# Two-layer decoder trunk: gate and up projections as block products with seven multiplications

## The chip, the cores and the metric

The kernel runs on one core of a Trainium2 chip. The metric is the device time of one execution in microseconds, as the median of several runs. Five engines work side by side: TensorE (PE, matmuls; its weight loads are listed as PEld), VectorE (DVE), ScalarE (ACT), GpSimd (POOL) and SyncE (SP), whose queue issues almost all the transfers of this kernel.

## The reference

The trunk has two layers on 1024 tokens of width 1024, in float32. Each layer is a mixer and a feed-forward block, each behind a root-mean-square norm and with its result added to x. The mixer of layer 0 is two gated convolutions, that of layer 1 a gated linear recurrence and a dilated attention. The feed-forward block is the part that the change is about:

```python
def conv_glu_ffn(h, w_gate, w_up, conv_w, conv_b, w_down):
    g = causal_dwconv(h @ w_gate, conv_w) + conv_b
    return (jax.nn.silu(g) * (h @ w_up)) @ w_down
```

with h of 1024 x 1024, `w_gate` and `w_up` of 1024 x 2816, `w_down` of 2816 x 1024, and a causal convolution of three taps over the tokens.

## The kernel before

Everything is kept channel-major: channels lie on the 128 partitions, tokens in the free dimension. A projection is therefore cut into tiles of 128 output channels, a contraction over 8 tiles of 128 channels (`KD`), and two halves of 512 tokens, since one PSUM bank holds 512 columns.

Each product is made of three matmuls. A float32 operand is split into a high part (a cast by ScalarE, L124 or L190) and a low part (a subtraction by VectorE, L125 or L191), and high x high, high x low and low x high are added up in PSUM (`in_part`, `in_full`, `out_pair`). All matmuls go through `mm` (L165). The weights are fetched in units of 128 x 1024 by `fetch` (L113) into two raw buffers and split by `load_w` into eight weight tiles.

`Norm` keeps x times the gain split in `hT`; 1 / rms is computed beside it (`stat`, `prep`, `spread`) as a row `br` that is multiplied into the results of the first projections.

A feed-forward layer (`ffn`, L317) goes over 22 channel tiles f. For each it runs the gate unit and the up unit (`in_unit`), then `evac` (L322): the multiplication by `br` (L324), bias and first tap (L325), two more taps (L301), silu (L327), again `br` (L328, on GpSimd), the multiplication by the up result (L329), and the split of the activation into two tiles of the g pool. The down projection is woven in: after each chunk of two tiles f, the activations of the chunk before are multiplied with their rows of `w_down` by eight `out_pair`, which add into x (L281). So neither activations nor x leave SBUF; only between layer 0 and layer 1 is x stored to `xscr` and read back later.

The order on each engine is not the order in which the lines are written. A planner at compile time goes through all instructions, knows their dependences and priorities (an earlier line has the higher one), and puts the next ready one on each engine. A buffer pool with n slots lets the planner run ahead by n tiles. Pools that are closed give their place to pools opened later, and a new tile then waits for the last use of the tile that it lies on.

Of the kernel before, what the change touches and what calls it, by code (L numbers as in the profile page):

```python
# [29 lines left out]
# columns of the packed per-channel parameters  # L30
# [11 lines left out]
# order of the packed weight units  # L42
# [9 lines left out]
def trunk(ctx, tc, x, wpk, par, wgate, masks, ident, out):  # L52
# [3 lines left out]
    hpool = ctx.enter_context(tc.tile_pool(name="hpool", bufs=4))  # L56
    wpool = ctx.enter_context(tc.tile_pool(name="wpool", bufs=8))
    rpool = ctx.enter_context(tc.tile_pool(name="rpool", bufs=2))
    gpool = ctx.enter_context(tc.tile_pool(name="gpool", bufs=8))
    xpool = ctx.enter_context(tc.tile_pool(name="xpool", bufs=2))  # L60
    dpool = ctx.enter_context(tc.tile_pool(name="dpool", bufs=1, space=bass.MemoryType.DRAM))
# [6 lines left out]

    def g_tile(dt=F32):
        return gpool.tile([P, 1024], dt, tag="g", name=nm("g"))  # L70
# [14 lines left out]

    def open_e(st):
        E["e"] = st.enter_context(tc.tile_pool(name=nm("ep"), bufs=7, reuse_waits="tile"))
        E["b"] = st.enter_context(tc.tile_pool(name=nm("bp"), bufs=1, reuse_waits="tile"))

    def open_psum(st, mm_bufs, tr_bufs):  # L90
        E["mm"] = st.enter_context(
            tc.tile_pool(name=nm("mmp"), bufs=mm_bufs, space=bass.MemoryType.PSUM, reuse_waits="tile"))
        trp = st.enter_context(
            tc.tile_pool(name=nm("trp"), bufs=tr_bufs, space=bass.MemoryType.PSUM, reuse_waits="tile"))
        E["tr"] = lambda shape: trp.tile(shape, F32, tag="tr", name=nm("tr"))

# [7 lines left out]

    st = ExitStack()
    open_e(st)
    open_psum(st, 3, 2)

    raws = {}

    def fetch(u):
        raw = rpool.tile([P, 1024], F32, tag="raw", name=nm("raw"))
        nc.sync.dma_start(raw, wpk[u])  # L113
        return raw

    def w_tile():
        return wpool.tile([P, 1024], F32R, tag="w", name=nm("w"))
# [16 lines left out]
    raw0 = raws[U_EVIN] = rpool.tile([P, 1024], F32, tag="raw", name=nm("raw"))  # L134
# [21 lines left out]
    xscr = dpool.tile([2, P, KD, 512], F32, name="xscr")  # L156
# [3 lines left out]
    def new_hT():  # L160
        return [[hpool.tile([P, KD, 512], F32R, tag="hT", name=nm("hT")) for _ in range(2)]
                for _ in range(2)]
# [5 lines left out]
    def colvec(sm, nt, scale):  # L168
        """(scale * column sums + eps) ** -0.5 by token, tokens on partitions."""
# [12 lines left out]
    class Norm:  # L182
        def __init__(self, n, xs, hT):
            self.n, self.xs, self.hT, self.acc, self.rs, self.br = n, xs, hT, {}, {}, None

        def turn(self, hf, ks):
            hi, lo = self.hT[hf]
            for k in ks:
                xk, g = self.xs[hf][:, k, :], pc("ng", 8 * self.n + k)
                nc.scalar.activation(hi[:, k, :], xk, AF.Identity, scale=g)  # L190
                nc.vector.scalar_tensor_tensor(  # L191
                    lo[:, k, :], xk, g, hi[:, k, :].bitcast(F32), ALU.mult, ALU.subtract)

        def stat(self, hf, cp):
            sq = e_tile()
            nc.scalar.activation(sq.rearrange("p (a b) -> p a b", a=2),  # L196
                                 self.xs[hf][:, 2 * cp:2 * cp + 2, :], AF.Square)
            if cp == 0:
                self.acc[hf] = sq
            else:  # L200
                nc.gpsimd.tensor_add(self.acc[hf], self.acc[hf], sq)  # L201

        def prep(self, hf):
            sm = self.acc[hf]
            nc.gpsimd.tensor_add(sm[:, 0:512], sm[:, 0:512], sm[:, 512:1024])
            self.rs[hf] = rs = colvec(sm, 4, 1.0 / D)
            self.dg = e_tile()
            diag(self.dg, rs, 4)

        def spread(self, hf):  # L210
            ps = tr_tile([P, 512])
            mm(ps, one1, self.dg[:, 0:512], True, True)
            if hf == 0:
                self.br = E["b"].tile([P, 1024], F32, tag="br", name=nm("br"))
            nc.scalar.copy(self.br[:, hf * 512:(hf + 1) * 512], ps)

        def stats(self):
            for hf in range(2):
                for cp in range(4):
                    self.stat(hf, cp)  # L220

        def hooks(self):
            """By half, unit and contraction tile of the first projections."""
            return {(0, 2, 4): lambda: self.prep(0), (1, 0, 0): lambda: self.spread(0),
                    (1, 0, 4): lambda: self.prep(1), (1, 1, 2): lambda: self.spread(1)}

# [1 line left out]
    def in_part(ps, w, hT, hf, hook):  # L228
        wh, wl = w
        hi, lo = hT[hf]  # L230
        o = ps[:, hf * 512:(hf + 1) * 512]
        for k in range(KD):
            hook(k)
            c = slice(k * P, (k + 1) * P)
            mm(o, wh[:, c], hi[:, k, :], k == 0, False)
            mm(o, wl[:, c], hi[:, k, :], False, False)
            mm(o, wh[:, c], lo[:, k, :], False, k == KD - 1)

    def in_full(ps, w, hT):
        wh, wl = w  # L240
        for k in range(KD):
            c = slice(k * P, (k + 1) * P)
            for hf in range(2):
                o = ps[:, hf * 512:(hf + 1) * 512]
                mm(o, wh[:, c], hT[hf][0][:, k, :], k == 0, False)
                mm(o, wh[:, c], hT[hf][1][:, k, :], False, False)
            for hf in range(2):
                o = ps[:, hf * 512:(hf + 1) * 512]
                mm(o, wl[:, c], hT[hf][0][:, k, :], False, k == KD - 1)

    def in_first(units, norm):
        hooks = norm.hooks()
# [30 lines left out]
    def out_one(xs, hf, c, t0, n, parts):  # L283
        o = mm_tile()[:, :n]
        t = slice(hf * 512 + t0, hf * 512 + t0 + n)
        cs = slice(c * P, (c + 1) * P)
        for i, ((ah, al), (wh, wl)) in enumerate(parts):
            mm(o, wh[:, cs], ah[:, t], i == 0, False)
            mm(o, wh[:, cs], al[:, t], False, False)
            mm(o, wl[:, cs], ah[:, t], False, i == len(parts) - 1)  # L290
        xv = xs[hf][:, c, t0:t0 + n]
        nc.vector.tensor_add(xv, xv, o)

    def out_all(xs, parts):
        for hf in range(2):
            for cp in range(4):
                out_pair(xs, hf, cp, parts)

# [3 lines left out]

    def r_tile():
        return g_tile(F32R)

    def out_norm(xs, parts, norm, before=None):
        """Last output projection of a phase with the next phase's norm behind it."""
        for hf in range(2):
            for cp in range(4):
                out_pair(xs, hf, cp, parts)  # L310
                if before:
                    before(hf, cp)
                norm.turn(hf, (2 * cp, 2 * cp + 1))
                norm.stat(hf, cp)

# [1 line left out]
    def ffn(layer, xs, norm, finish):  # L317
        hT = norm.hT
        u0 = U_F[layer]
        chunks = [list(range(2 * c, 2 * c + 2)) for c in range(9)] + [list(range(18, 22))]  # L320

        def evac(f, pg, pu):  # L322
            g, t = e_tile(), e_tile()
            nc.vector.tensor_mul(g, norm.br, pg)  # L324
            nc.scalar.activation(t, g, AF.Identity, bias=pc(f"fb{layer}", f), scale=pc(f"fw{layer}", 44 + f))  # L325
            conv_rest(t, g, lambda i: pc(f"fw{layer}", 22 * i + f), 3)
            nc.scalar.activation(t, t, AF.Silu)  # L327
            nc.gpsimd.tensor_mul(t, t, norm.br)  # L328
            nc.vector.tensor_mul(t, t, pu)  # L329
            return split(t, r_tile)  # L330

        def down(acts):
            return [(a, load_w(u0 + 44 + f)) for f, a in acts.items()]

        pend = None
        for ci, ch in enumerate(chunks):
            acts = {}
            for n, f in enumerate(ch):
                if ci == 0 and n == 0:
                    pg, pu, pg1 = in_first([u0 + 0, u0 + 1, u0 + 2], norm)  # L340
                    acts[0] = evac(0, pg, pu)
                elif ci == 0:
                    acts[1] = evac(1, pg1, in_unit(u0 + 3, hT))
                else:
                    pg = in_unit(u0 + 2 * f, hT)
                    pu = in_unit(u0 + 2 * f + 1, hT)
                    acts[f] = evac(f, pg, pu)
                if n == 1 and pend is not None:
                    out_all(xs, down(pend))
            pend = acts  # L350
        return finish(down(pend))
# [702 lines left out]
```

## Time and profile before

| | us |
|---|---|
| median of 3 runs | 2322.82 (2322.39 to 2324.06) |
| span of the profiled execution | 2320.8 |
| TensorE busy in it | 2238.9 |
| VectorE busy | 1245.4 |
| ScalarE busy | 667.4 |
| GpSimd busy | 452.8 |

The profiled execution has no run time of its own in the page; its span, from the first to the last instruction, is 2.0 us under the median, and the difference is what lies around the instructions. In the span, the first mixer lasts to about 402 us, the first feed-forward to about 1123 us, the mixer of layer 1 to about 1585 us, and the second feed-forward to the end.

How to read it: the busy time of an engine is the time in which at least one of its instructions was in flight. The chain that ended last is followed back from the last instruction, at each step to what released it. A bracket behind a row says how long the engine was idle before it and what ended that.

### The profile page before, as it was taken

What the parts mean: (1) busy time and instruction counts of PE and PEld (TensorE: products, weight loads), DVE (VectorE), ACT (ScalarE), POOL (GpSimd) and SP (SyncE); (2) the same over time, 40 slices, a digit from 0 to 9 for tenths busy, and PEclk for the clock granted to TensorE, in tenths of its full rate; (3) what the DMA queues carried; (4) which work ended last, traced back from release to release, by engine and by line L of the source; (5) the groups of instructions that cost most, each with busy time, mean ns of one, the idle gap of its engine ahead of it and who ended that gap; (6) DMA issues with size and microseconds to landing.
All of it is one profiled execution on the core that took longest, in us unless ns stands there. A gap on an engine that the chain in (4) does not pass through costs nothing.

```text
span 2320.8 us, 26137 instructions
## 1 busy us (share of the span) xinstructions
PE 2238.9 (96%) x11064; PEld 1888.4 (81%) x11064; DVE 1245.4 (54%) x1383; ACT 667.4 (29%) x928; POOL 452.8 (20%) x235
## 2 busy tenths in 40 slices
PE   7876899999999999999999999999999999999999
PEld 6654788888888888888889999888788888888887
DVE  6999966544444444444587242565544444444443
ACT  5332225212122112113373444443312112122110
POOL 4556532100000000001225120224100000000000
PEclk9987999999999999999999999999999999999999
DMA  4100111111111111111312210221111111111111
GB/s 156 34 28 27 39 34 55 61 49 37 55 55 46 54 47 46 53 48 64 109 46 72 80 60 30 92 83 46 55 46 46 55 46 44 48 55 46 55 46 73
DMA packets 42884, 128.63 MB, mean 55 GB/s; under 512 B 4880, under 2 KB 13840, under 8 KB 42768
## 3 DMA queue, kind: packets, MB, share of 16 engines
q1 hardware_dynamic: 42480, 126.82, 16.7%
q8 instruction: 87, 1.43, 0.2%
q14 instruction: 29, 0.24, 0.0%
q10 hardware_dynamic: 288, 0.15, 0.0%
HBM read 114.30 MB, written 12.65 MB: 55 GB/s over the span
## 4 chain that ended last, share of the span: by engine, by line
PE 88%; DVE 9%; issue 2%; ACT 1%; DMA 0%; POOL 0%; ACTq 0%; DVEq 0%
PE mm L165 73%; PE pq L165 9%; DVE e L370 6%; PE S L165 2%; PE pl L165 2%; PE tr L165 1%; DVE w L125 1%; PE pa L165 1%; PE pt L741 1%; PE pt L648 0%; ACT e L196 0%; DVE g L364 0%; DVE e L389 0%; DMA x<-xscr 0%; DVE hT L191 0%
## 5 line engine op out<-in xcount | busy, mean ns | idle before, releaser
L165 PE MATMUL mm<-hT,w 128*128 128x512 f32 x5568 | 1291.6, 393 | 72.3 <-DVE e L427 30.9
L165 PEld LDWEIGHTS mm<-hT,w 128*128 128x128 f32 x5568 | 1053.5, 190 | 299.5 <-issue 64.7
L165 PE MATMUL mm<-g,w 128*128 128x512 f32 (+1 forms) x2316 | 527.3, 388 | 0.0
L165 PEld LDWEIGHTS mm<-g,w 128*128 128x128 f32 x2316 | 433.2, 188 | 90.2 <-issue 0.7
L124 ACT CAST w<-raw 128x1024 fp32r<-128x1024 f32 (+1 forms) x191 | 199.7, 1047 | 951.9 <-PE mm L165 893.2
L328 POOL TENSOR_TENSOR e<-e,br 128x1024 f32<-128x1024 f32 x44 | 105.3, 2394 | 1196.4 <-ACT e L327 1162.5
L281 DVE TENSOR_TENSOR x<-x,mm 128x1024 f32<-128x1024 f32 x175 | 213.2, 1220 | 216.5 <-PE mm L165 216.5
L125 DVE TENSOR_TENSOR w<-raw,w 128x1024 fp32r<-128x1024 f32 (+1 forms) x191 | 251.4, 1317 | 54.0 <-ACT w L124 53.9
L165 PE MATMUL pq<-w,hT 128*128 128x256 f32 x1728 | 222.5, 287 | 1.4 <-ACT k L622 1.4
L324 DVE TENSOR_TENSOR e<-br,mm 128x1024 f32<-128x1024 f32 x44 | 53.7, 1221 | 307.7 <-PE mm L165 300.3
L165 PEld LDWEIGHTS pq<-w,hT 128*128 128x128 f32 x1728 | 211.9, 192 | 4.5 <-ACT k L622 1.8
L329 DVE TENSOR_TENSOR e<-e,mm 128x1024 f32<-128x1024 f32 x44 | 53.7, 1221 | 237.2 <-PE mm L165 232.3
L370 DVE SCALAR_TENSOR_TENSOR e<-g,parm,e 128x1013 f32<-128x1013 f32 (+20 forms) x84 | 173.5, 2109 | 1.5 <-ACT e L366 1.3
L301 DVE SCALAR_TENSOR_TENSOR e<-e,parm,e 128x1023 f32<-128x1023 f32 x96 | 125.2, 1305 | 8.9 <-ACT e L325 7.3
L385 POOL TENSOR_TENSOR g<-g,e 128x1022 f32<-128x1022 f32 (+7 forms) x32 | 104.1, 3254 | 53.0 <-ACT e L384 51.8
L201 POOL TENSOR_TENSOR e<-e,e 128x1024 f32<-128x1024 f32 x24 | 63.2, 2635 | 123.5 <-ACT e L196 122.9
L327 ACT ACTIVATE e<-e 128x1024 f32<-128x1024 f32 x44 | 46.7, 1061 | 112.3 <-DVE e L301 112.3
L191 DVE SCALAR_TENSOR_TENSOR hT<-x,parm,hT 128x512 fp32r<-128x512 f32 x64 | 64.5, 1045 | 11.1 <-ACT hT L190 11.1
L124 ACT CAST g<-e 128x1024 fp32r<-128x1024 f32 x48 | 50.5, 1052 | 65.7 <-DVE e L329 37.5
L325 ACT ACTIVATE e<-e,parm 128x1024 f32<-128x1024 f32 x44 | 54.8, 1247 | 27.7 <-DVE e L324 27.7
L125 DVE TENSOR_TENSOR g<-e,g 128x1024 fp32r<-128x1024 f32 x48 | 60.7, 1265 | 2.2 <-ACT g L124 2.2
L190 ACT ACTIVATE hT<-x,parm 128x512 fp32r<-128x512 f32 x64 | 42.4, 712 | 42.8 <-DVE x L281 28.7
(152 smaller groups left out, 1272.4 us busy)
## 6 DMA issues: line engine op xcount, KB each, us to landing
raw<-in_wpk_dram SPq DMA_DIRECT2D x191, 512.0 KB, 3.5
xscr<-x SPq DMA_DIRECT2D x8, 512.0 KB, 2.6
x<-xscr SPq DMA_DIRECT2D x8, 512.0 KB, 5.5
x<-in_x_dram SPq DMA_DIRECT2D x7, 512.0 KB, 9.0
out_dram<-x SPq DMA_DIRECT2D x7, 512.0 KB, 2.6
R<-ascr SPq DMA_DIRECT2D x8, 264.0 KB, 2.8
vscr<-k SPq DMA_DIRECT2D x8, 256.0 KB, 2.6
ascr<-res SPq DMA_DIRECT2D x16, 66.0 KB, 2.1
```

The source lines that it names most:

```text
L124: nc.scalar.copy(hi[:, p], raw[:, p])
L125: last_lo[0] = nc.vector.tensor_sub(lo[:, p], raw[:, p], hi[:, p].bitcast(F32))
L165: nc.tensor.matmul(o, lhsT=l, rhs=r, start=st, stop=sp)
L191: nc.vector.scalar_tensor_tensor(lo[:, k, :], xk, g, hi[:, k, :].bitcast(F32), ALU.mult, ALU.subtract)
L201: nc.gpsimd.tensor_add(self.acc[hf], self.acc[hf], sq)
L281: nc.vector.tensor_add(xv, xv, ps.rearrange("p (a b) -> p a b", a=2))
L301: nc.vector.scalar_tensor_tensor(t[:, j:], src[:, :S - j], ws(n - 1 - j), t[:, j:], ALU.mult, ALU.add)
L324: nc.vector.tensor_mul(g, norm.br, pg)
L325: nc.scalar.activation(t, g, AF.Identity, bias=pc(f"fb{layer}", f), scale=pc(f"fw{layer}", 44 + f))
L328: nc.gpsimd.tensor_mul(t, t, norm.br)
L370: return lambda: nc.vector.scalar_tensor_tensor(u[:, s:], t[:, :S - s], pc("cfw", 4 * (30 - s) + j), u[:, s:], ALU.mult, ALU.add)
L385: nc.gpsimd.tensor_add(box["a"][:, s:], box["a"][:, s:], tmp[:, s:])
```

## The change

Gate and up of one tile f are seen as one 2 x 2 block matrix: rows are gate and up, columns the lower and upper half of the contraction (A11, A12 of gate, A21, A22 of up). The operand is a 2 x 2 block matrix too: contraction halves by token halves (B11, B21 of the first 512 tokens, B12, B22 of the second). The product needs eight block products; the change forms it from seven, after Strassen and Winograd, with sums of blocks: S1 to S4 of weights, formed on VectorE for each f, and T1 to T4 of operands, formed once a layer. Each block product is 12 matmuls of 512 columns. Results are partly added up in the banks, partly copied out and added on VectorE.

The activations of each f are stored to DRAM (`fscr`). After all 22, the down projection is a phase of its own in three passes over f, of six, six and four banks (`PASSES`); each pass loads the weight columns and activations that it needs and splits them together. x is stored to `xscr` ahead of each feed-forward and read back in its passes. Norm statistics go by single channel tiles; the weight, raw, e and g pools are closed during a feed-forward and others are opened in their place.

```diff
+class Fast(Norm):
+        def put(self, hf, c):
+            k, low = c % 4, c < 4
+            x0, x1 = self.xs[0], self.xs[hf]
+            g = self.gain(c)
+            if hf == 0:
+                self.split("B11" if low else "B21", k, x0[:, c, :], g)
+            elif low:
+                t1 = x0[:, k, :]
+                nc.vector.tensor_sub(t1, x1[:, k, :], t1)
+                nc.scalar.activation(t1, t1, AF.Identity, scale=g)
+                self.split("T1", k, t1)
+            else:
+                t = x0[:, k, :]
+                b22 = t_tile()
+                nc.scalar.activation(b22, x1[:, c, :], AF.Identity, scale=g)
+                nc.vector.tensor_sub(t, b22, t)
+                self.split("T2", k, t)
+                t3 = x1[:, k, :]
+                self.split("B22", k, b22)
+                nc.vector.scalar_tensor_tensor(t3, t3, self.gain(k), b22, ALU.mult, ALU.subtract)
+                self.split("T3", k, t3)
+                t4 = x0[:, c, :]
+                nc.vector.scalar_tensor_tensor(t4, t4, g, t, ALU.mult, ALU.subtract)
+                self.split("T4", k, t4)
...
+    def product(bank, w, b, first):
+        bh, bl = b
+        for k in range(4):
+            c = slice(k * P, (k + 1) * P)
+            for j, (l, r) in enumerate(((w[:, 0, c], bh), (w[:, 0, c], bl), (w[:, 1, c], bh))):
+                nc.tensor.matmul(bank, lhsT=l, rhs=r[:, k, :], start=first and k + j == 0,
+                                 stop=k == 3 and j == 2, skip_group_check=True)
+
+    def gate_up(layer, f, norm):
+        w, op, br = Weights(U_F[layer] + 2 * f), norm.op, norm.br
+        X, Y, Z = u_tile(), u_tile(), u_tile()
...
+        product(X, w.get("A11"), op["B11"], True)
+        nc.scalar.copy(s1, X)
+        yield
+        product(Y, w.get("A12"), op["B21"], True)
+        nc.vector.tensor_add(g[:, lo], s1, Y)
+        yield
+        product(Z, w.get("S1"), op["T1"], True)
+        nc.scalar.copy(s5, Z)
+        yield
+        product(X, w.get("S2"), op["T2"], False)
+        nc.scalar.copy(s6, X)
+        yield
+        product(Z, w.get("S4"), op["B22"], False)
+        nc.vector.tensor_add(g[:, hi], s6, Z)
+        nc.vector.tensor_mul(g, g, norm.br)
+        nc.scalar.activation(t, g, AF.Identity, bias=pc(f"fb{layer}", f), scale=pc(f"fw{layer}", 44 + f))
+        conv_rest(t, g, lambda i: pc(f"fw{layer}", 22 * i + f), 3)
+        nc.scalar.activation(t, t, AF.Silu)
+        nc.vector.tensor_mul(t, t, norm.br)
+        yield
+        product(X, w.get("S3"), op["T3"], False)
+        nc.vector.tensor_add(s5, s5, X)
+        yield
+        product(X, w.get("A22"), op["T4"], False)
+        nc.vector.tensor_mul(a[:, lo], t[:, lo], X)
+        nc.vector.tensor_mul(a[:, hi], t[:, hi], s5)
+        nc.sync.dma_start(fscr[layer][f], a)
+        yield
...
+        order = [0, 0, 1, 1, 0, 1, 0, 0, 0, 1, 0, 1, 1]
+        for f in range(2, NF):
+            order += [f, f - 1] + [f] * 5
+        order.append(NF - 1)
...
+            for f in range(NF):
...
+                raw = E["r2"].tile([P, 2048], F32, tag="raw", name=nm("raw"))
...
+                wh, wl = [al().rearrange("p a b -> p (a b)")[:, 0:nw + na] for _ in range(2)]
+                nc.scalar.copy(wh, raw[:, 0:nw + na])
+                nc.vector.tensor_sub(wl, raw[:, 0:nw + na], wh.bitcast(F32))
+                for j, (hf, c) in enumerate(keys):
...
+                    mm(banks[j], wh[:, cs], wh[:, ts], f == 0, False)
+                    mm(banks[j], wh[:, cs], wl[:, ts], False, False)
+                    mm(banks[j], wl[:, cs], wh[:, ts], False, f == NF - 1)
```

The slots are: 2 raw buffers of 8 KB a partition, 6 split weights, 5 sums, 6 operand tiles of the new pool and 8 of the old one, 6 banks for X, Y and Z or for a pass, 2 working tiles of x's size for `g`, `t` and the copies. In the mixer of layer 1 the pool for `k2` goes from 4 slots to 3 and `res` from 3 to 2.

## Rows read from the trace of the kernel before

**Rows 1.** The page: busy time per engine, and TensorE in tenths by 40 slices.

```profile
PE 2238.9 (96%) x11064; PEld 1888.4 (81%) x11064; DVE 1245.4 (54%) x1383; ACT 667.4 (29%) x928; POOL 452.8 (20%) x235
...
PE   7876899999999999999999999999999999999999
```

**Rows 2.** Windows by stage: length, busy of five engines, clock, DMA share, GB/s.

```profile
30.00:263.00 233.00, 174.83 (x732) 141.62 (x731) 219.95 (x146) 67.24 (x64) 132.72 (x48) 0.88 0.11 37
402.14:1123.88 721.74, 721.74 (x3189) 597.14 (x3190) 330.22 (x289) 163.83 (x162) 73.44 (x32) 1.00 0.16 54
...
1631.81:2317.69 685.88, 685.87 (x3036) 568.40 (x3036) 300.03 (x250) 137.34 (x126) 52.63 (x22) 1.00 0.16 51
```

**Rows 3.** The chain that ended last, its two longest pieces: start, length, what.

```profile
430.39 692.48 PE mm L165 x3055
...
1631.81 685.88 PE mm L165 x3036
```

**Rows 4.** Groups by line and shape: busy us, mean ns, idle before and releaser.

```profile
L165 PE MATMUL mm<-hT,w 128*128 128x512 f32 x5568 | 1291.6, 393 | 72.3 <-DVE e L427 30.9 <-DVE e L361 22.1 <-ACT w L124 8.0
...
L328 POOL TENSOR_TENSOR e<-e,br 128x1024 f32<-128x1024 f32 x44 | 105.3, 2394 | 1196.4 <-ACT e L327 1162.5 <-issue 33.9
...
L325 ACT ACTIVATE e<-e,parm 128x1024 f32<-128x1024 f32 x44 | 54.8, 1247 | 27.7 <-DVE e L324 27.7
...
L324 DVE TENSOR_TENSOR e<-br,mm 128x1024 f32<-128x1024 f32 x44 | 53.7, 1221 | 307.7 <-PE mm L165 300.3 <-ACT br L215 7.4
...
L327 ACT ACTIVATE e<-e 128x1024 f32<-128x1024 f32 x44 | 46.7, 1061 | 112.3 <-DVE e L301 112.3
...
L743 ACT COPY pT<-pt 128x512 f32<-128x512 f32 x24 | 14.0, 583 | 21.7 <-PE pt L741 21.5
...
L205 POOL TENSOR_TENSOR e<-e 128x512 f32<-128x512 f32 x8 | 12.7, 1591 | 0.6
...
L874 DVE TENSOR_TENSOR x<-x,pl 128x512 f32<-128x512 f32 x16 | 10.9, 686 | 18.7 <-PE pl L165 15.7 <-DMA x<-xscr 3.0
```

**Rows 5.** Timeline of VectorE: start, length, line, operation, count; in feed-forward, then attention.

```profile
720.35 1.22 DVE L324 TENSOR_TENSOR e<-br,mm 128x1024 f32<-128x1024 f32 x1 [7.89 <-PE mm L165]
721.49 1.22 DVE L125 TENSOR_TENSOR w<-raw,w 128x1024 fp32r<-128x1024 f32 x1
722.88 2.60 DVE L301 SCALAR_TENSOR_TENSOR e<-e,parm,e 128x1023 f32<-128x1023 f32 x2 [0.18 <-ACT e L325]
...
1561.24 1.29 DVE L874 TENSOR_TENSOR x<-x,pl 128x512 f32<-128x512 f32 x2 [3.02 <-DMA x<-xscr]
```

**Rows 6.** DMA issues: count, KB each, median us from issue to landing.

```profile
raw<-in_wpk_dram SPq DMA_DIRECT2D x191, 512.0 KB, 3.5
...
x<-xscr SPq DMA_DIRECT2D x8, 512.0 KB, 5.5
```

**Rows 7.** Timeline of SP and ScalarE at the start of layer 1: a load and its cast.

```profile
1120.94 0.33 SPq L113 DMA_DIRECT2D raw<-in_wpk_dram  x1
...
1124.58 1.05 ACT L124 CAST w<-raw 128x1024 fp32r<-128x1024 f32 x1 [2.74 <-DMA raw<-in_wpk_dram]
```

**Rows 8.** Windows: the first loads, a pause of TensorE, the two feed-forward starts.

```profile
18.00:20.00 2.00, 0.54 (x1) 0.50 (x2) 2.00 (x2) 2.00 (x4) 1.92 (x2) 0.50 0.19 76
12.00:14.00 2.00, 2.00 (x7) 1.42 (x5) 2.00 (x2) 2.00 (x4) 1.92 (x2) 1.00 1.03 414
402.00:412.00 10.00, 10.00 (x47) 8.28 (x46) 10.00 (x15) 6.80 (x10) 5.38 (x3) 1.00 0.32 92
1585.00:1632.00 47.00, 44.80 (x232) 37.30 (x231) 27.14 (x33) 15.59 (x20) 17.38 (x9) 1.00 0.21 68
```

**Rows 9.** Timeline of the first mixer: the second half's spread and the first evacuation.

```profile
51.49 1.02 PE L165 MATMUL tr<-e,one 128*128 128x512 f32 x2
...
53.17 1.22 DVE L361 TENSOR_TENSOR e<-br,mm 128x1024 f32<-128x1024 f32 x1 [3.48 <-ACT br L215]
```

More of the change, by code (lines that the diff above doesn't have):

```diff
@@ L211, in spread @@
             ps = tr_tile([P, 512])
-            mm(ps, one1, self.dg[:, 0:512], True, True)
-            if hf == 0:
[L214 to L225, printed above, removed]
+            mm(ps, one1, self.dg[hf][:, 0:512], True, True)
@@ L301, in conv_rest, with rows4 @@
             nc.vector.scalar_tensor_tensor(t[:, j:], src[:, :S - j], ws(n - 1 - j), t[:, j:], ALU.mult, ALU.add)
+    def rows4():
+        t = [h_tile().rearrange("p (a b) c -> p a (b c)", b=2) for _ in range(2)]
+        return [t[j // 2][:, j % 2, :] for j in range(4)]
     def r_tile():
         return g_tile(F32R)
[L306 to L314, printed above, removed]
@@ L317, in ffn @@
[L317 to L343, printed above, removed]
-                else:
[L345 to L351, printed above, removed]
@@ L355, in mixer0 @@
+    def mixer0(xs, norm, hooks):
         hT = norm.hT
@@ L468, in mixer0 @@
         pr = colsum(one1, dg)
[L469 to L470 removed]
+        vh, vl = rows4(), rows4()
         ycf = []
@@ L550, in scan @@
             return r
-        pxs = in_first([U_LRU + j for j in range(3)], norm)
+        pxs = in_first([U_LRU + j for j in range(3)], norm,
+                       {(1, 0, 4): lambda: norm.prep(1), (1, 1, 2): lambda: norm.spread(1)})
         cv = [conv(j, pxs[j]) for j in range(3)]
@@ L910, in attention @@
             if n in (7, 8):
-                norm.turn(0, range(4 * (n - 7), 4 * (n - 7) + 4))
+                for c in range(4 * (n - 7), 4 * (n - 7) + 4):
+                    keep(0, c)
+                    norm.stat(0, c)
+                    norm.put(0, c)
             if 1 <= n <= 8:
@@ L915, in attention @@
                 tn[n - 2]()
+            if n == 9:
+                norm.prep(0)
         for cp in range(4):
             out_att(3, cp)
-            norm.turn(1, (2 * cp, 2 * cp + 1))
-        return norm
-    norm = Norm(0, xs, new_hT())
+            if cp == 0:
+                norm.spread(0)
+            for c in (2 * cp, 2 * cp + 1):
+                keep(1, c)
+                norm.stat(1, c)
+        return norm
+    norm = Plain(0, xs)
+    for hf in range(2):
+        for c in range(KD):
+            norm.put(hf, c)
@@ L923, in trunk, with second @@
+    for c in range(KD):
+        norm.stat(0, c)
+    def second():
+        norm.spread(0)
+        for c in range(KD):
+            norm.stat(1, c)
+    parts = mixer0(xs, norm, {(0, 2, 4): lambda: norm.prep(0), (1, 0, 0): second,
+                              (1, 1, 4): lambda: norm.prep(1), (1, 2, 2): lambda: norm.spread(1)})
+    norm2 = Fast(2, xs)
+    keep = spill(xs, 0)
     for hf in range(2):
         for cp in range(4):
-            norm.turn(hf, (2 * cp, 2 * cp + 1))
-    norm.stats()
@@ new lines, in trunk, with ffn_phase, to_mixer1, f @@
+            for c in (2 * cp, 2 * cp + 1):
+                keep(hf, c)
+                norm2.stat(hf, c)
+                if hf == 0:
+                    norm2.put(hf, c)
+    ste.close()
+    stw.close()
+    def ffn_phase(layer, norm, make, between):
+        st = ExitStack()
+        open_ffn(st)
+        for c in range(KD):
+            norm.put(1, c)
+        ffn(layer, norm, xscr[2 * layer], make, between)
+        st.close()
+    box = {}
+    def to_mixer1(xs):
+        n, keep = Plain(1, xs), spill(xs, 1)
+        box["n"] = n
+        def f(hf, c):
+            keep(hf, c)
+            n.stat(hf, c)
+            n.put(hf, c)
+        return f
```

324 lines of the change are left out of this document (209 added, 115 removed).

## The prediction

> **What bounds the kernel now.** I read the page's busy shares first: TensorE is busy 96% of the span and in nearly every slice [rows 1]. A busy share does not say who sets the pace, so next come the windows by stage. In both feed-forward stages TensorE is busy for the whole window, 721.74 of 721.74 us and 685.87 of 685.88 us, while VectorE is busy under half [rows 2]. Only the first mixer (30 to 263 us) is bound by VectorE, 219.95 of 233 us [rows 2]. Third, the chain of work that ended last has two long pieces made of nothing but matmuls: 692.48 us with 3055 of them, and 685.88 us with 3036 [rows 3]. That gives the price this case turns on: 692.48 / 3055 = 0.2267 us from one 512-column matmul to the next. The mean of one, 393 ns [rows 4], is how long a matmul is in flight, neighbours overlap in it, and it must not be used as a price.
>
> A feed-forward layer has 22 channel tiles f. Each costs 96 matmuls in gate and up (2 units x 8 contraction tiles x 2 halves x 3 parts) and 48 in down: 144 x 22 = 3168, or 718 us a layer.
>
> **The multiplications.** Seven products of 12 matmuls (4 contraction tiles x 3 parts) replace 96 by 84 for each f. Down keeps 16 banks x 22 x 3 = 1056. So 12 x 44 = 528 matmuls go, of the same shape, at 0.2267 us: **-119.7 us**. This is on the path for its full length, since TensorE never waits there [rows 2]. A product now takes 2.72 us and an f 19.0 us.
>
> **VectorE and ScalarE under seven products.** Per f VectorE has sixteen 512-wide operations (4 weight sums, 7 low parts, 5 sums or products with a bank), 2 of 1024 and the two convolution taps. Back to back, 512 wide costs about 0.60 us (a pair ends after 1.29), 1024 wide 1.14 us from start to start, the taps 2.60 together [rows 5]: 9.6 + 2.3 + 2.6 = 14.5 us of 19.0, 76%, against 46% before [rows 2]. The product of t with br moves from GpSimd (2.39 us [rows 4]) to VectorE and is counted in it. ScalarE has seven casts and three copies out of banks at about 0.6 us (a copy is 583 ns), bias 1.25 and silu 1.06 [rows 4]: 8.3 us. Neither becomes the bound by its sum.
>
> The new waits are tighter, though. Four reads of a bank stand between two products that add into it. The copies of Z and of the second X have one product of 2.72 us to hide a 0.58 us copy: free. The tight one is s5 += X, read after the product with S3 and needed before the last product of f; the first product of f+1 is placed between. If VectorE took its work as written, that sum would stand behind the chain g, br, bias, taps, silu, br: 0.69 + 1.22 + 1.25 + 2.60 + 1.06 + 1.22 = 8.0 us [rows 4, 5] after the end of the fifth product, then 0.69 itself, against two products, 5.44 us: 3.3 us for each f, 145 us in all. Behind it TensorE would hold the product with A22, and everything after it. But the order in the trace is not the written one: between the multiplication and the taps the planner put a weight's low part into the gap [rows 5]. The same filling can put the sum into the 1.25 us bias gap or the silu gap, and TensorE can take the second product of f+1 first. Bounds 0 and 145, nearest to the row that shows filling: I take 0.2 us x 44 = **+9**. By the Trainium skill (TensorE: Matmul & The Clock Gate, Part 2, step 1) matmuls stay in program order and only weight loads are pulled ahead; no run here shows an overtaking. It makes any such wait a wait of all that follows.
>
> **The start of each feed-forward.** Before, TensorE is gapless from the mixer into the first layer and loses 47.0 - 44.8 = 2.2 us at the second [rows 8]. Now the five operand pairs are 36 VectorE operations for the second half (2 for each low channel tile, 7 for each high one), 21.6 us; that engine was already full there, 10.00 of 10 us [rows 8]. Ten products, 27 us, lie between the first and the last that needs them, so half of this hides. The new weight buffers lie on tiles of the phase before, so the load of 1 MB may wait for the last squares' sums on GpSimd (two of 1.59 us [rows 4] after an addition and a square, 4.5 us), then land (3.64 us for half of it [rows 7] plus 1.27 at 414 GB/s [rows 8]) and be split, 1.2: 10.6 us. A TensorE gap also costs clock: after the pause at 16 to 20 us the granted clock is 0.50, the 1.2 GHz level [rows 8]. Bounds 0 (loads early) and 22 each; I take 10, twice, less the 2.2: **+18**.
>
> **Down in three passes.** Per f a pass loads weight columns and activations, casts and subtracts, and has two raw buffers. TensorE takes 18 x 0.2267 = 4.08 us for each f (12: 2.72 in the third pass). The loop of one buffer is landing, cast, subtraction. A 512 KB load reaches its cast 3.64 us after issue [rows 7]; more bytes go at 414 GB/s [rows 8]; a second or third issue adds up to 0.33 us [rows 7]. Cast and subtraction are 1.05 and 1.22 us for 1024 columns [rows 5, 7]. First pass, 640 KB: 4.3 + 1.3 + 1.5 = 7.1, half of it 3.6: hidden. Second, 896 KB: 5.3 + 1.8 + 2.1 = 9.2, 4.6 a step, +0.54 x 22 = 12. Third, 512 KB: 4.0 + 2.3 = 6.2, 3.1 a step, +0.40 x 22 = 9. Without the extra issues the two are 5 and 5; I take 15. Reloading x for the second half, 2 MB at 414 GB/s, stands ahead of these loads on SP's queue: 5. That is 20 a layer, **+40**; bounds 0 (all hidden) and, at the 5.5 us that four loads at once took [rows 6], 75 a layer. The row of single loads is the nearer one, since mostly one buffer is in flight.
>
> The Trainium skill (DMA: Bandwidth & Descriptors, Anatomy of one DMA) gives 2.0 us plus bytes at 436 GB/s: 3.2 us for 512 KB where the row has 3.5 [rows 6]. By it the second pass hides and the third pays 2 us: the sum would be some 25 us lower, an estimate from that page.
>
> **Small edges.** In the first mixer the second half's 1/rms comes one projection later; its first evacuation waited for it already (53.17 after 51.49) [rows 9], and the VectorE-bound stage shifts by about 3 us. LRU weights lie on down's last operands, so they are split after the pass ends: 1.05 + 1.22 + landing left over, 3.5. Between gate/up and down the last four banks and fscr: 1 each, and 11 each if reads wait for the last write; the activations' stores (0.5 MB every 19 us, waiting on SP's queue for the last product, with the load for f+2 behind them, due 19 us later) hide. Layer 0's norm work between passes 3, the attention's smaller buffers 2 (res has two slots where three blocks were in flight). Together **+13**, bounds 4 and 45. The added spills and stores run beside 0.16 DMA share [rows 2].
>
> **Sum.** -119.7 + 9 + 18 + 40 + 13 = -39.7. The profiled span is 2320.8 us and the median of the runs 2322.8, 2.0 us more. 2320.8 - 39.7 + 2.0 = **2283 us**, own range 2255 to 2310.
>
> **The rivals.** (a) All hidden: loads prefetched, starts covered, chain filled; 4 + 10 + 0 + 6 is left of the costs: 2223 us. For it: the planner kept 690 us without a gap [rows 3]. (b) The sum behind the taps only, 0.69 + 1.22 + 1.25 + 2.60 + 0.69 = 6.45 against 5.44 us, 1.0 us x 44 in place of 9: 2318 us. For it: the taps are ready at about the same moment. (c) Slower: the two-buffer loop of the passes at a 5.5 us landing, 150 in place of 40: 2393 us. It decides from about 4.5 us for 512 KB, where the loops cost 80. For it: pass two moves 896 KB each 4 us, four times the mean rate of the stage, 54 GB/s [rows 2]; against: the queue reached 414 GB/s at the start [rows 8]. (d) The whole chain before the sum, 145 in place of 9: 2419 us; against it stands the filled gap. That fewer matmuls run is plain from the code.
>
> **Chances.** Forecast 0.50, (a) 0.20, (b) 0.10, (c) 0.14, (d) 0.06. A measurement tells about 0.2%, 4.6 us, from no change; half of (b) lies in that band or beside it. Faster 0.73, within 0.06, slower 0.21. The range takes in (b), most of (a) and the start of (c): 2225 to 2355.
>
> **What would show it.** Right: about 10536 matmuls in place of 11064, gate/up windows of 19.0 us per f with TensorE full, and gaps of 5 to 15 us at the two starts. Passes two and three at 4.3 to 4.6 and 2.9 to 3.1 us a step, with ScalarE's cast waiting for the load. For (b) or (d): TensorE idle before the product with A22 in each f, released by VectorE's s5 sum. For (c): casts waiting for loads with steps over 5 us. Wrong altogether if matmuls in the products are further apart than 0.2267 us.

## The result and the profile after

The changed kernel takes 2287.82 us (median of 4 runs, 2284.78 to 2289.5) against 2323.44 us in the same comparison: ratio 0.9844, 95% interval 0.983 to 0.9858, 35.6 us less. The forecast was 2283. The profiled execution has a span of 2285.1 us, 35.7 us below the span of before.

The page of the changed kernel, busy time per engine and TensorE in tenths by 40 slices; beside it [rows 1]:

```profile
PE 2152.5 (94%) x10524; PEld 1796.1 (79%) x10524; DVE 1547.5 (68%) x1969; ACT 928.5 (41%) x1397; POOL 358.2 (16%) x215
...
PE   7875899799999999999899999997899999999999
```

540 records of matmuls fewer, where 528 go by the code. VectorE has 302 us more, and TensorE has dents that it did not have: slice 8 (400 to 457 us), slice 20 (1085 to 1142) and slices 28 and 29 (1542 to 1657), which hold the two starts and the change to the mixer of layer 1.

The chain that ended last, its two longest pieces (start, length, what); beside it [rows 3]:

```profile
437.41 394.42 PE u L415 x1740
...
1625.15 394.42 PE u L415 x1740
```

394.42 / 1740 = 0.2267 us: a matmul costs what it cost before, and gate and up have no gap.

Windows by stage of the changed kernel: length, busy of PE, PEld, DVE, ACT and POOL with their counts, then granted clock, DMA share and GB/s; beside them [rows 2, 8]. They are, in order: the first start, gate and up, the three passes, and in layer 1 the start, gate and up, and the second and third pass.

```profile
402.00:437.40 35.40, 23.27 (x83) 18.30 (x84) 35.22 (x57) 21.63 (x40) 4.26 (x3) 0.76 0.20 75
437.40:831.80 394.40, 394.40 (x1742) 326.56 (x1741) 308.28 (x416) 165.54 (x251) 0.00 (x0) 1.00 0.25 86
831.80:943.00 111.20, 111.20 (x493) 92.02 (x491) 55.72 (x44) 42.31 (x40) 9.00 (x5) 1.00 0.65 215
943.00:1040.00 97.00, 90.06 (x378) 68.68 (x377) 47.65 (x32) 39.70 (x33) 3.04 (x2) 1.00 0.61 199
1040.00:1100.80 60.80, 57.61 (x235) 44.27 (x233) 29.92 (x30) 20.98 (x23) 6.43 (x4) 0.97 0.48 156
1585.00:1625.20 40.20, 24.28 (x91) 19.07 (x90) 38.88 (x59) 24.58 (x46) 10.86 (x7) 0.70 0.24 92
1625.20:2019.60 394.40, 394.40 (x1741) 326.69 (x1740) 309.43 (x417) 168.03 (x253) 0.00 (x0) 1.00 0.25 87
...
2131.00:2225.00 94.00, 89.95 (x380) 69.73 (x379) 44.86 (x28) 34.00 (x22) 0.00 (x0) 1.00 0.64 212
2225.00:2280.40 55.40, 53.73 (x222) 40.06 (x221) 23.08 (x20) 18.88 (x18) 0.00 (x0) 1.00 0.48 160
```

What is lost in a stretch is its length less its matmuls at 0.2267 us (the busy time hides small gaps, since neighbours overlap). So the cost of the change can be set against the prediction's terms:

| term | predicted | measured | how |
|---|---|---|---|
| multiplications | -119.7 | -119.7 | 528 x 0.2267 us, the price as before |
| VectorE chain and s5 | +9 | 0 | gate and up without a gap |
| the two starts | +18 | +32 | 19.0 + 22.7 lost, less 3.9 + 5.7 lost in the two feed-forward layers before |
| passes of down | +40 | +36 | 269.0 and 260.8 us for 1090 matmuls each, 247.1 |
| small edges | +13 | +17 | start of the recurrence 8.9, attention 5.5, the first mixer 0.8, the end 1.5 |
| sum | -39.7 | -35 | spans: -35.7 |

Where the starts lose: pieces of the chain back from 440 us, in layer 0 (start, length, what).

```profile
397.57 4.34 PE mm L205 x19
...
404.83 1.27 POOL acc L239
...
406.18 1.61 POOL acc L239
...
407.80 4.89 DMA raw<-in_wpk_dram
...
412.72 1.14 ACT s L406 x2
413.86 0.52 ACT hT L255
414.38 3.12 ACT hx L255 x6
417.50 0.53 ACT s L406
...
418.07 18.48 PE u L415 x68
```

And TensorE's timeline there, with the idle time before each and what ended it:

```profile
407.83 1.87 PE L205 MATMUL tr<-one,acc 128*128 128x1 f32 x8 [5.93 <-POOL acc L239]
413.39 2.07 PE L415 MATMUL u<-hT,s 128*128 128x512 f32 x4 [3.69 <-ACT s L406]
418.07 2.07 PE L415 MATMUL u<-hT,s 128*128 128x512 f32 x4 [2.61 <-ACT s L406]
```

The old projections end at 401.9. The first weight load is issued at 407.80, right when GpSimd's last addition of squares ends, lands in 4.89 us, and the second cast of a weight stands behind six casts of operands on ScalarE. Full rows of products run from 418.07, the first of them slowly: 18.48 us for 68 matmuls, 3.1 us over their price, with a granted clock of 0.55 at 415 to 425 us, after the gap (0.50 is the lower level, 1.2 GHz). Layer 1 shows the same: load issued at 1595.23, products from 1605.75.

### The profile page after: what moved, and what is told of

The parts are those of the page before. It is cut to its first block, busy times and chain, and to the rows that moved or that the text cites. A ratio compares the mean times of both kernels' runs of the same rounds, so it can differ in the third digit from the quotient of the medians.

```text
span 2285.1 us, 26922 instructions
## 1 busy us (share of the span) xinstructions
PE 2152.5 (94%) x10524; PEld 1796.1 (79%) x10524; DVE 1547.5 (68%) x1969; ACT 928.5 (41%) x1397; POOL 358.2 (16%) x215
## 4 chain that ended last, share of the span: by engine, by line
PE 71%; DVE 13%; DMA 8%; ACT 4%; issue 2%; SPq 1%; POOL 1%; ACTq 0%; DVEq 0%; POOLq 0%
PE u L415 37%; PE mm L205 11%; PE pq L205 9%; PE u L205 8%; DMA raw<-fscr 7%; DVE e L535 6%; DVE hx L503 3%; ACT hx L502 2%; PE S L205 2%; PE pl L205 2%; DVE w L156 1%; SPq L497 1%; PE tr L205 1%; DMA raw<-in_wpk_dram 1%; DVE hT L259 1%
## 5 line engine op out<-in xcount | busy, mean ns | idle before, releaser
L415 PE MATMUL u<-hT,s 128*128 128x512 f32 x2112 | 508.3, 393 | 12.8 <-ACT s L406 12.8
L415 PEld LDWEIGHTS u<-hT,s 128*128 128x128 f32 x2112 | 400.6, 190 | 98.0 <-ACT s L406 14.5
L205 PE MATMUL mm<-hT,w 128*128 128x512 f32 x1536 | 372.7, 403 | 69.8 <-DVE e L592 31.3
L205 PEld LDWEIGHTS mm<-hT,w 128*128 128x128 f32 x1536 | 298.9, 196 | 139.3 <-issue 63.9
L503 DVE TENSOR_TENSOR hx<-raw,hx 128x1792 fp32r<-128x1792 f32 (+2 forms) x128 | 203.3, 1591 | 272.1 <-ACT hx L502 271.9
L415 PE MATMUL u<-hx,s 128*128 128x512 f32 x1584 | 382.9, 390 | 0.0
L205 PE MATMUL u<-hx,hx 128*128 128x512 f32 x1360 | 371.0, 394 | 9.5 <-DVE hx L503 9.0
L415 PEld LDWEIGHTS u<-hx,s 128*128 128x128 f32 x1584 | 297.8, 188 | 62.8 <-issue 1.0
L205 PEld LDWEIGHTS u<-hx,hx 128*128 128x128 f32 x1360 | 252.8, 188 | 76.4 <-DVE hx L503 24.9
L205 PE MATMUL u<-hx 128*128 128x512 f32 x680 | 214.5, 395 | 6.3 <-ACT hx L502 6.2
L205 PEld LDWEIGHTS u<-hx 128*128 128x128 f32 x680 | 126.5, 189 | 40.1 <-ACT hx L502 13.7
```

Of the source, the lines that this page charges most:

```text
L205: nc.tensor.matmul(o, lhsT=l, rhs=r, start=st, stop=sp)
L415: nc.tensor.matmul(bank, lhsT=l, rhs=r[:, k, :], start=first and k + j == 0, stop=k == 3 and j == 2, skip_group_check=True)
L503: nc.vector.tensor_sub(wl, raw[:, 0:nw + na], wh.bitcast(F32))
```

## The experiments

All are edits of the changed kernel, and their times stand beside its 2287.82 us.

**Are the multiplications the gain?** The same phases, stores and passes with eight plain products for each f and no sums:

```diff
-        product(X, w.get("A11"), op["B11"], True)
+        wa, wb = w.get("A11"), w.get("A12")
+        product(X, wa, op["B11"], True)
...
+        product(V, wc, op["T1"], True)
...
+        product(V, wd, op["B22"], False)
```

> The phases, stores and passes of the changed kernel stay, but gate and up are formed by eight plain block products that add up in two banks each, with no sums of weights or operands. Theory one, the gain is the multiplications: 528 matmuls at 0.2267 us come back, +119.7 us, and the starts give back at most some 10 us each because VectorE has 16 in place of 36 operations there: 2388 to 2408 us, slower than before by 3 to 4%. Theory two, the gain comes from the new phases: the time stays between 2288 and 2320 us.

Measured: 2398.79 us, ratio to before 1.0322 (1.0307 to 1.0338). Its gate and up in layer 0 (window, columns as above):

```profile
414.70:894.30 479.60, 479.60 (x2113) 397.25 (x2113) 204.49 (x242) 106.91 (x134) 0.00 (x0) 1.00 0.21 77
```

So the new staging alone makes the kernel 75.5 us slower, and seven products in place of eight win 111 us, 9 less than the 119.7 of the matmuls. The starts lose about 28 us here (401.8 to 414.7 and 1643.4 to 1658.8) in place of 41.7, and the rest of the two layers some 5 us more, which makes up the 9. The operands need no sums here, and TensorE's order is another; which of the two shortens the starts this run does not tell. Down as phases would be a plain loss without the multiplications.

**The passes: a loop over two buffers?** The changed kernel's ScalarE, VectorE and TensorE in the second pass:

```profile
958.58 1.69 ACT L502 CAST hx<-raw 128x1792 fp32r<-128x1792 f32 x1 [5.25 <-DMA raw<-fscr]
...
960.30 2.02 DVE L503 TENSOR_TENSOR hx<-raw,hx 128x1792 fp32r<-128x1792 f32 x1 [4.92 <-ACT hx L502]
...
962.38 3.06 PE L205 MATMUL u<-hx,hx 128*128 128x512 f32 x12 [0.39 <-DVE hx L503]
```

Load, cast, subtraction, product: each waits for the one before, with the transfer at the head. The edit gives the loop a third buffer, and takes the place from the split weights:

```diff
-        for key, bufs in (("hx", 6), ("s", 6), ("r2", 2), ("tp", 5)):
+        for key, bufs in (("hx", 6), ("s", 4), ("r2", 3), ("tp", 5)):
```

> Three raw buffers in place of two, four split weights in place of six, all else as in the changed kernel. Theory one, the passes of the down projection are bound by the loop of load, cast and subtraction over two buffers: a third takes the step of the second pass from about 4.66 to 4.08 us and of the third from about 3.0 to 2.72, the passes lose under 10 us of 36, and the time is about 2260 us. Theory two, they are bound by the transfers' rate or by ScalarE and VectorE in turn: the steps stay and the time is 2284 to 2292 us. If four split weights are too few, the gate and up windows show gaps and the time is longer.

Measured: 2258.18 us, ratio 0.9716 (0.97 to 0.9732). Windows of the second pass in both layers, and of the third in layer 1:

```profile
943.00:1040.00 97.00, 96.53 (x428) 79.35 (x427) 59.11 (x44) 44.86 (x39) 8.60 (x6) 1.00 0.66 219
...
2131.00:2225.00 94.00, 94.00 (x417) 77.82 (x416) 46.89 (x33) 36.89 (x28) 0.00 (x0) 1.00 0.66 214
2225.00:2250.00 25.00, 25.00 (x112) 20.71 (x111) 9.80 (x8) 7.65 (x8) 0.00 (x0) 1.00 0.39 129
```

The passes run without gaps. From the end of the long row of gate and up to the end of the passes there are 255.1 and 252.5 us for 1113 products each, 252.3: they lose 2.8 and 0.2 us in place of 21.9 and 13.7. So of the 36 us, 33 were the loop, and 3 are left for the entry to down, the reload of x and the changes of pass. The DMA share stays near what it was (0.66 against 0.61 and 0.64), so the queue was not the limit; the wait for a free buffer was. The starts lose no less than in the changed kernel (43 us), though the first load is issued at 403.13 and 1573.08 here.

**Is the s5 sum hidden because it is filled in?** The sum is held back until the last multiplication by `br`, the full chain of rival (d):

```diff
-        nc.vector.tensor_mul(t, t, norm.br)
+        last = nc.vector.tensor_mul(t, t, norm.br).ins
...
-        nc.vector.tensor_add(s5, s5, X)
+        with tc.issue_after(last):
+            nc.vector.tensor_add(s5, s5, X)
```

> The sum s5 + X, which the last product of each f waits for, is queued on VectorE behind the multiplication with br that ends the activation's chain. Theory one, this wait sets the pace once the order is the written one: 3.3 us for each of 44 f, 145 us, about 2430 us. Theory two, the planner fills the wait with the matmuls of the next f, which need nothing of it: within 10 us of 2288.

Measured: 2290.74 us (two runs, 2289.53 and 2291.95), and gate and up stay full:

```profile
435.70:830.00 394.30, 394.30 (x1741) 326.62 (x1740) 306.81 (x415) 166.86 (x252) 0.00 (x0) 1.00 0.24 85
```

In the changed kernel the sum lies between the two taps in 22 of the 44 f and before them in 20, so the planner does fill it in, as the prediction thought possible. In most f it starts 4.2 to 6.6 us before the multiplication by `br`; held back, it starts 1.14 us after it, and there is still no wait. The reason is TensorE's order in the traces. As written, one product stands between the product with S3 and that with A22. In a steady f of the changed kernel there are 28 matmuls between them (6.3 us: two products and a third of the next), and with the sum held back 51 (11.6 us). The planner moves the reader of the sum, not only the sum.

**The starts: is it the place of the weight buffers?** The pools are opened in another order, so that the first raw buffers lie on tiles that come free early:

```diff
-        for key, bufs in (("hx", 6), ("s", 6), ("r2", 2), ("tp", 5)):
+        for key, bufs in (("hx", 4), ("r2", 2), ("s", 6), ("hy", 2), ("tp", 5)):
...
+        hxn[0] += 1
+        return E["hy" if hxn[0] % 6 in (5, 0) else "hx"].tile([P, 4, 512], F32R, tag="hx", name=nm("hx"))
```

> The pools of the feed-forward are laid out in another order (four operand tiles, raw buffers, split weights, the other two operand tiles, sums; same sizes), so that the first weight loads lie on tiles that the mixers finished long before, not on those of the last norm statistics. Theory one, the starts wait for the load: the changed kernel's first products come 11.5 us (layer 0) and 15.2 us (layer 1) after the last projection because the load is issued only when GpSimd's last addition ends; without that wait the two starts lose about 8 us each instead of 19.0 and 22.7, and the time is about 2288 - 25 = 2263 us. Theory two, the starts are bound by VectorE, which is busy 35.2 of the 35.4 us of the first start: the products come earlier but then wait for operands and weights, no more than 5 us is won at each start, and the time is 2278 to 2288 us.

Measured: 2279.66 us (2278.41 to 2286.25), ratio 0.9817 (0.9802 to 0.9832). The theory of placement gets 8 of its 25 us, and the time lies in the range of theory two. In layer 0 the products now start at 407.10, directly behind the projections, and TensorE stops later instead (its waits: for the diagonal of 1/rms 4.13 us, for weights 2.83 and 1.98). In the traced run, the slowest of the four, the lost time of both starts goes from 41.7 to 35.4 us. So the load's wait ended last in the changed kernel, with others close behind it. Part of the gain is paid in the mixer before. The first load is issued at 369.06 there, VectorE waits for that weight's cast ahead of an addition to x that TensorE in turn waits for; in the changed kernel it does not stand there:

```profile
374.57 0.69 DVE L410 TENSOR_TENSOR s<-raw,s 128x512 fp32r<-128x512 f32 x1 [5.54 <-ACT s L409]
...
376.44 5.86 PE L208 MATMUL mm<-hT,w 128*128 128x512 f32 x18 [2.23 <-DVE x L371]
```

**Is VectorE, full in the start, what ends last in the changed kernel?** VectorE's low parts of T1 to T4 are left out; in their place ScalarE writes the rounded copy a second time:

```diff
+            if name in ("T1", "T2", "T3", "T4"):
+                nc.scalar.copy(hi[:, k, :], src)
+                nc.scalar.copy(lo[:, k, :], src)
+                return
```

> The changed kernel with its pool order, but the low parts of the four operand differences T1 to T4 written by ScalarE as a second rounded copy (that part of the computation is changed), so that 16 of VectorE's 36 subtractions, 9.6 us, leave VectorE in each of the two starts. The trace of the changed kernel shows VectorE busy 35.22 of 35.40 us there, but TensorE standing until 418.07 for a weight whose load was issued at 407.80. Theory 'the load ends last, VectorE close behind': nothing or little is won, 2284 to 2290 us, and TensorE's first full row of products still begins at 417 to 419 us. Theory 'a full VectorE sets the start': 10 to 19 us less, 2269 to 2278 us.

Measured: 2291.07 us, ratio 0.986 (0.9844 to 0.9877), 1 us above the range of the first theory. VectorE is no longer full in the same window (24.59 in place of 35.22 us), and nothing is won. TensorE still stands for GpSimd's sums (8.0 us) and then for a weight, so that its first products begin at 418.18; a full row runs only from 424.10, where 417 to 419 was expected, because the diagonal came late. Window and TensorE's row:

```profile
402.00:437.40 35.40, 19.86 (x68) 14.86 (x67) 24.59 (x40) 28.62 (x54) 5.08 (x4) 0.71 0.20 74
```

```profile
418.18 2.07 PE L419 MATMUL u<-hT,s 128*128 128x512 f32 x4 [4.76 <-ACT s L410]
```

So taking work off an engine that is busy 35.22 of 35.40 us wins nothing as long as the load is late. ScalarE, which took the work, is fuller (28.62 in place of 21.63 us), so a small gain may be hidden in it.

**Are GpSimd's additions the root?** The second half's squares are added up on VectorE:

```diff
-                nc.gpsimd.tensor_add(self.acc[hf], self.acc[hf], sq)
+                eng = nc.vector if hf == 1 and isinstance(self, Fast) else nc.gpsimd
+                eng.tensor_add(self.acc[hf], self.acc[hf], sq)
```

> The changed kernel with the eight additions of the second half's squares on VectorE instead of GpSimd, in both feed-forward starts. In the changed kernel TensorE waited 5.9 and 9.4 us for those additions (their sum stands before the first products on TensorE), and the first weight load was issued only after the last of them, at 407.80 and 1595.23. Theory 'GpSimd's additions are the root of the late load': the load is issued 2 to 4 us earlier in layer 0 and 5 to 8 us earlier in layer 1, and the time falls by 5 to 10 us: 2278 to 2283 us. Theory 'the work only moves onto a VectorE that is full there': 8 x 0.60 = 4.8 us more on it in each start, and the time stays or grows: 2286 to 2296 us.

Measured: 2283.84 us (2279.16 to 2284.74), ratio 0.9823 (0.9806 to 0.9839), 4 us less. The load is issued only 0.3 and 1.4 us earlier (407.48, 1593.87), and TensorE waits 5.1 and 7.8 us for the additions in place of 5.9 and 9.4. The additions are one link of a chain from the last residual over the squares, and a faster link does not shorten the rest. The time lies between the two ranges.

**What is late next?** On the kernel with the other pool order (e1), 1/rms is taken three products earlier:

```diff
-            if n == 5:
+            if n == 2:
                 norm.prep(1)
```

> The pool order of e1_places, and besides the second half's sum of squares is turned into its 1/rms after the third product of the feed-forward instead of after the sixth. Rows of e1_places behind it: GpSimd's power of 128x4, 1.40 us in the changed kernel, took 6.21 us at 427.01 and 8.62 us at 1606.35, each in the middle of a row of VectorE subtractions, and TensorE waited 4.13 and 4.56 us for the diagonal that is made from it. Theory 'late 1/rms': it is taken early, outlasts little, and TensorE's waits of 4.1 and 4.6 us before that product go, with some of what stands behind them: about 2268 us (2262 to 2273). Theory 'VectorE alone sets the start': VectorE has the same work, the waits only move to other operands: 2276 to 2281 us.

Measured: 2278.28 us, ratio 0.9802 (0.9787 to 0.9816), no clear difference to e1, and in the range of the second theory. TensorE now waits longer at one place, since the spread of 1/rms stands earlier in its order while the diagonal stands where it stood in VectorE's:

```profile
428.54 2.07 PE L208 MATMUL tr<-tp,one 128*128 128x512 f32 x2 [11.71 <-DVE tp L223]
```

On top of that, the low parts of T1 to T4 are replaced by ScalarE's second copy again:

> e5_prep, but the low parts of the four operand differences T1 to T4 are written by ScalarE as a second rounded copy of the difference (so they are not the remainders: that part of the computation is changed), which takes 16 of VectorE's 36 subtractions of each start, 16 x 0.60 = 9.6 us, off VectorE. Theory 'VectorE sets the start': up to 9.6 us less in each of the two starts, 10 to 19 us below e5_prep. Theory 'loads and ScalarE's casts set it': no change or a little slower than e5_prep, since ScalarE gets 16 x 0.52 = 8.3 us more.

Measured: 2273.48 us (2270.31 to 2276.51), 4.8 us less than 2278.28 (2274.91 to 2279.53). The lost time of both starts goes from 36.8 to 29.5 us, and the wait for the diagonal from 11.7 to 6.56 in layer 0 and from 8.60 to 1.61 in layer 1. Here, where the first load of layer 0 comes in time, VectorE's work does cost, but a quarter of the 19 us that left it, under the range that was expected of a VectorE that sets the start.

**Both gains together.** Pool order, early 1/rms, three raw buffers:

> e5_prep and e3_raw3 together: pool order, early 1/rms, three raw buffers and four for the split weights. If the passes' loop and the start are separate costs, the two gains add: e5_prep less the 29.6 us of e3_raw3 (2287.8 - 2258.2), about 2238 to 2250 us. If the early loads of the start collide with the third raw buffer (it lies on other tiles of the phase before, and moves the others), the start loses its part again: about 2258 us.

Measured: 2252.03 us, ratio 0.969 (0.9675 to 0.9704). The gains nearly add up (26.3 of 29.6 us; the time is 2 us above the range expected for that), and this is the fastest of the kernels run: 72 us below the kernel before. A variant of it, and the three buffers with VectorE's additions, won nothing over it:

> e6_both with the four 128x128 diagonals of the second half's 1/rms made by ScalarE instead of VectorE, in both feed-forward starts. In e6_both TensorE waited 11.6 and 8.6 us in them for these diagonals, which stand on VectorE behind its row of subtractions. Theory 'the place in VectorE's order is the cost': most of the 20 us goes until the next operand is late, 2236 to 2244 us. Theory 'the operands of the following products are as late as the diagonal': the waits move to T1's or B22's parts, 2248 to 2254 us.

Measured: 2255.9 us, above both ranges. TensorE still waits 7.0 and 10.2 us for the diagonals, now from ScalarE.

> e12_vsq with the three raw buffers of e3_raw3. Here the load no longer waits for the additions (it was issued at 403.13 and 1573.08 in e3_raw3), but TensorE still waited 5.9 and 9.4 us for them. Theory 'TensorE's order makes the additions the cost': 6 to 12 us less than e3_raw3, 2246 to 2252 us. Theory 'VectorE is next and as late': 2256 to 2264 us.

Measured: 2254.74 us (2252.24 to 2258.85), 3.4 us below the kernel with three buffers, inside neither range.

So for the starts the runs show this much: at least two paths of about the same length lead to the first full row of products, the load with its casts and VectorE's row of operand parts and sums. With VectorE relieved and the load late (2291.07 us) nothing is won. With the load early and VectorE's work as it was, in the kernel with three buffers, the starts lose 43 us and VectorE is busy all the way from the projections to the first full row:

```profile
401.00:433.20 32.20, 19.80 (x63) 14.95 (x64) 32.20 (x52) 19.81 (x36) 4.26 (x3) 0.68 0.32 114
```

That kernel has four split weights in place of six, which may cost there too. Only with the load of layer 0 early, 1/rms early and VectorE relieved (2273.48 us) do the starts come down to 29.5 us. No single edit of the starts won more than 8 us. What a start costs with all of these gone stays open, and so does the part of GpSimd's power of 1/rms: a kernel with it on VectorE was planned and gave no time.

## Why the prediction was right

**The multiplications** were priced right, because the price was the step from one matmul to the next in the chain and not the 393 ns of one. The price held with VectorE at 78% in gate and up (308.28 of 394.40 us), near the 76% that the prediction counted.

**The chain and s5** were worth 0, not 9. The failed step is "the first product of f+1 is placed between": the sum took TensorE's order as written, while the order in the program is the planner's, which put two products and more there. The prediction names this way out (TensorE "can take the second product of f+1 first"), but kept 0.2 us for each f. Rivals (b) and (d) fell with it, (d) by experiment.

**The passes** are right in size and in the loop's mechanism, but not in their parts. Predicted were 4.6 and 3.1 us a step; from cast to cast, the second pass takes 4.7 and 4.5 us in the two layers and the third 3.2 and 3.0. From the first issue of a step to its cast it is 5.6 and 5.3 us in the second pass and 3.6 in the third (medians), where 5.3 and 4.0 were counted. The loops cost 33 us and not 30. The reload of x and the entry, counted at 10, cost next to nothing: the first pass is full from the end of gate and up on (111.20 of 111.20 us). Rival (c) did not come: it put the landing at 5.5 us, and the 512 KB of the second pass landed in 4.5, as the last of three transfers issued together. The prediction let (c) decide from 4.5 us on, for a load that starts with its step; this one is issued 0.8 us later, so that mark does not apply. The DMA issues of the changed kernel (count, KB each, median us to landing), beside [rows 6]:

```profile
raw<-in_wpk_dram SPq DMA_DIRECT2D x44, 1024.0 KB, 5.3
...
raw<-fscr SPq DMA_DIRECT2D x88, 256.0 KB, 3.5
...
raw<-fscr SPq DMA_DIRECT2D x44, 512.0 KB, 4.5
```

The Trainium skill's formula (DMA: Bandwidth & Descriptors, Anatomy of one DMA), by which the second pass would have been hidden, is fitted there to transfers that GpSimd issues; SyncE issues these. It gives 4.4 us for the first of these rows, where 5.3 was measured; the second pass did pay, 13 us of 97 in layer 0 and 8 of 94 in layer 1. The measured rows decide.

**The starts** were mis-sized: 32 in place of 18. The two starts lose 41.7 us where 20 were taken, and what was lost before was put at 2.2, from busy time, which hides small gaps, where it was 9.6. The named path was there, a load of 1 MB that waits for GpSimd's sums. The 10 us taken for a start are near each of its two parts alone, half of VectorE's 21.6 us and the 10.6 us of the load, as if one covered the other. In the changed kernel's chain the links of the load come one after the other: 5.9 us until the sums, 5.6 for load and first cast, 4.7 more for the second cast behind operand casts, and 3.1 at a lower clock; in layer 1 another 3.5 for the sums. The prediction did not lay them end to end, and it gave the clock no term. Nor is the load alone the cost: VectorE's row is about as long, as the experiments show.

**The edges** came to 17 for 13. The start of the recurrence was 8.9 us and not 3.5. TensorE first stands for GpSimd's sums there, but the load of the recurrence's weights ended later: it was issued 1.7 us after the last product, behind the stores of x, and landed after 5.98 us, where the prediction had 3.5 for cast, subtraction and the rest of the landing. The chain that ended last in the changed kernel, and then TensorE's timeline:

```profile
1102.52 5.98 DMA raw<-in_wpk_dram
...
1108.58 1.05 ACT w L155
```

```profile
1107.29 1.87 PE L205 MATMUL tr<-one,acc 128*128 128x1 f32 x8 [6.50 <-POOL acc L239]
1109.68 0.79 PE L205 MATMUL mm<-hT,w 128*128 128x512 f32 x1 [0.52 <-ACT w L155]
```

The errors have both signs (-9, +14, -4, +4) and nearly cancel, so the total is nearer than its terms deserve; that much of the hit is luck. The other side of the forecast, the chance of slower, was a real one: with eight products the same staging was slower by 3.2%.

## What to carry to other kernels

Price fewer multiplications at the step between matmuls, and then look for the loss at the edges of the new phases, where buffers, statistics and casts line up in series: add those links end to end. A loop of load, cast, subtraction and product over two buffers that is 10 to 16% over the price of its matmuls (here in the second and third pass) is cheaply mended by a third buffer, where the queue has room (here the share was 0.66 afterwards). A full engine is not yet the bound: take work off it and see whether the wait moves, and where nothing moves, take two waits away together.

## What the runs showed of the hardware

GpSimd's operation can last many times as long beside a row of VectorE's. Its power of 128 x 4 takes 1.02 to 2.00 us everywhere in the changed kernel; in the kernel with early 1/rms it took 8.02 us in layer 1. GpSimd's row, and VectorE's in the same stretch:

```profile
1599.63 8.02 POOL L218 TENSOR_TENSOR rs<-rs,nhalf 128x4 f32<-128x4 f32 x1 [12.02 <-DVE rs L217]
```

```profile
1602.48 2.48 DVE L259 TENSOR_TENSOR hx<-x,hx 128x512 fp32r<-128x512 f32 x4
1604.89 1.88 DVE L259 TENSOR_TENSOR hT<-x,hT 128x512 fp32r<-128x512 f32 x3
1607.68 0.87 DVE L223 TENSOR_SCALAR tp<-idt,rs 128x128 f32<-128x128 f32 x4 [0.91 <-POOL rs L218]
```

VectorE subtracts back to back from 1599.47 to 1606.77, and GpSimd's operation ends at 1607.65, 0.9 us after the row, about its own duration. In the kernel with the other pool order the same happened twice, 6.21 and 8.62 us, both ending 0.9 us after VectorE's row. With the row taken away it does not happen: in the kernel that differs from the one with early 1/rms only in the low parts that leave VectorE, the same operation in layer 1 took

```profile
1600.83 1.02 POOL L218 TENSOR_TENSOR rs<-rs,nhalf 128x4 f32<-128x4 f32 x1 [13.02 <-DVE rs L217]
```

The Trainium skill (SBUF — State Buffer, Who interferes with whom) states that a VectorE instruction with two inputs in SBUF contends with a GpSimd instruction that reads SBUF, and calls such contention an exclusive lock; these rows agree. It does not say why GpSimd found no turn between two of these subtractions, while in the changed kernel the same operation took 1.40 us among two-input operations of VectorE. The rows hold one hint: where VectorE's row has a SCALAR_TENSOR_TENSOR in it, GpSimd's power ended about 0.95 us after that one began (411.51 and 412.46 in the changed kernel, 421.55 and 422.50 in layer 0 of the kernel with early 1/rms). No run tried this apart, and why stays open.
